# An encoder block with expert retrieval on one core: preparing the operands of the dense stage's products one tile earlier, with a third buffer for one pair of halves

## Chip, core and metric

One NeuronCore of a Trainium2 chip runs the whole program. The metric is the device time of one execution in microseconds. The profile is that of one further execution, taken by the hardware profiler; its times are counted from the first instruction of the span. Engines are called as in the profile: PE (TensorE matmul; PEld is its weight load), DVE (VectorE), ACT (ScalarE), POOL (GpSimd) and SP (SyncE, which here only issues transfers).

## The reference

One layer on 512 tokens of width 1024: modulation from `c`, an input projection, dilated and differential attention, gates, an output projection, and then PEER, a feed-forward part that picks 16 of 16384 single-neuron experts for each of 8 heads and each token. PEER is where the change lies:

```
q = (xc @ w_query).reshape(PEER_CHUNK, PEER_HEADS, 2, PEER_HALF)
... top 16 of the keys of either half, then of their 256 sums ...
eidx = e1 * PEER_N_KEYS + e2
gate = jax.nn.softmax(top, axis=-1)
u = expert_u[eidx]
vv = expert_v[eidx]
act = jax.nn.gelu(jnp.einsum('td,thkd->thk', xc, u).astype(jnp.float32), approximate=False)
wts = (gate * act).astype(xc.dtype)
return jnp.einsum('thk,thkd->td', wts, vv)
```

## The kernel before

The kernel computes PEER in two ways side by side. For 128 of the tokens it gathers the chosen rows of `expert_u` and `expert_v` from memory: 256 indirect transfers of 128 rows (512 KB each), issued by POOL into four buffers `gat`; DVE uses each once, as a dot product (`gscr`, L1065) or as a weighted sum (`acc`, L1077). For the other 384 tokens it works densely over all 16384 experts in 128 tiles of 128 experts: gelu(h2 u) for every expert, times the gate (zero for the experts that a token did not choose), times V. A matmul of two f32 operands is made of three: each operand is split into a high half, which ACT makes by a copy, and a low half, which DVE or POOL makes by subtracting (`split`, L91 and L92; `hi, lo` for weights, `ah, al` for activations), and PE multiplies high by high, high by low and low by high.

**The dense stage** is the loop at L1207, in the order of the list `order`: eight tiles whose activations are computed in the stage (e from 64 on: `stage_s` loads their `uT`, splits it, has PE do 24 products `pj`, and ACT apply gelu into `am`), then eight tiles whose activations were computed earlier in the program and stored (e below 64: `stage_s` loads `am` from `gls`), and so on, eight times. In this text tiles are numbered 0 to 127 in that order, and U is the `uT` of a tile and V its `expert_v`. `stage_s` runs LEAD = 4 tiles ahead, so that the 24 products of U for tile n+4 stand before the 18 products `y` of tile n. So the products of tiles 12 to 19, 28 to 35, 44 to 51 and so on come with a U each (here: a heavy stretch), and those of tiles 4 to 11, 20 to 27, 36 to 43 and so on without (a light stretch). The gathers and their uses are spread over the loop by `run_jobs(done)` at the end of each turn, twice as many for a tile with e from 64 on.

What a turn does for its own tile, before its products: multiply `am` by the gates `gch` (DVE, L1212), split the result into `ah` and `al` (two buffers each), load V (`w4`), and split it into `vh` and `vl`. V and U share the pool of `w4`: five buffers of either half, three of `raw`. `am` has four buffers. `gch` holds the gates of eight tiles (1.5 MB, two buffers) and is loaded by `stage_s` at the first tile of eight.

Five things set the order. PE, DVE, ACT and SP each take their instructions in the order that a scheduler of the language made of the source when the program was built, by the source's order and its own estimates; each engine then waits at an instruction until its operands and buffers are there. POOL is under `manual_schedule` in this loop and takes its instructions in the source's order. A load waits on SP for its buffer, and what is behind it on SP waits too.

Of the kernel before, what the change touches and what calls it, by code (L numbers as in the profile page):

```python
# [16 lines left out]
F32R = mybir.dt.float32r  # L17
# [5 lines left out]
OP = mybir.AluOpType  # L23
# [872 lines left out]
def peer(K, A, out):  # L896
    nc, cst, gen, Pool = K.nc, K.cst, K.gen, K.Pool
    small, f2, mm3, split, ident = K.small, K.f2, K.mm3, K.split, K.ident
    h2tok = K.h2tok
    gd, gls = A['gd'], A['gls']  # L900
    ND, NS = 384, 64
# [4 lines left out]
    pw, w4 = K.pw, K.w4  # L906
# [8 lines left out]
    def ptr():  # L915
        return pe_.tile([128, 512], F32, name="pt", bufs=2)

    def pg():
        return pe_.tile([128, 512], F32, name="pg", bufs=2)
# [49 lines left out]
    for c in range(4):  # L969
        pieces = []  # L970
        for k in range(0, 8, 2):
            raw, hi, lo = w4(wq[:, k:k + 2, 512 * c:512 * c + 512])
# [3 lines left out]
        for hc in range(2):  # L976
            h = 2 * c + hc
# [110 lines left out]
    def run_jobs(done):  # L1088
        while jobs and njobs - len(jobs) < done:
            jobs.pop(0)()  # L1090
# [14 lines left out]
    for b, a in enumerate(DT):  # L1105
# [3 lines left out]
        for n, t in enumerate(slots(gt, a)):  # L1109
            p = ptr()  # L1110
# [16 lines left out]
        for t0 in range(0, 128, T):  # L1127
# [15 lines left out]
            for q in range(0, T, 4):  # L1143
                p = pg()
# [21 lines left out]
    v = A['expert_v'].rearrange("(e p) d -> e p d", p=128)  # L1166
    py = Pool("py", space=PSUM)
    ys = [[py.tile([128, 512], F32, name=f"y{b}{n}") for n in range(2)] for b in range(3)]
    lp = Pool("main")
    gch, ams = {}, {}  # L1170

    def stage_s(e):
        if e % 8 == 0:
            gch[e // 8] = lp.tile([128, 12, 8, 32], F32, name="gch", bufs=2)
            nc.sync.dma_start(gch[e // 8].rearrange("p h e t -> p h (e t)"),
                              gd[e // 32][:, e // 8 % 4].rearrange("h p e t -> p h (e t)"))
        am = ams[e] = pa.tile([128, ND], F32, name="am", bufs=4)
        if e < NS:
            nc.sync.dma_start(am, gls[e])
        else:  # L1180
            gelu_s(e, pmat(), am, nc.gpsimd if e % 2 == 0 else nc.vector)


    order = []
# [3 lines left out]
    order = [8 * c + i for c in order for i in range(8)]  # L1188
# [3 lines left out]
    def residual(a):  # L1192
        for n in range(2):
            ns = slice(n * 512, n * 512 + 512)
            y = lp.tile([128, 512], F32, name="yo", bufs=6)
            nc.vector.tensor_tensor(y, acc[:, ns] if a == 0 else ys[a - 1][n], K.g2[:, ns], op=OP.mult)
            (nc.gpsimd if a in PR else nc.vector).tensor_tensor(y, y, xr[a][:, ns], op=OP.add)
            (nc.scalar if n else nc.sync).dma_start(ov[:, a, ns], y)
# [5 lines left out]
    pool_order = K.tc.manual_schedule(engines={mybir.EngineType.Pool})  # L1204
    pool_order.__enter__()
    done = float(J0)
    for n_, e in enumerate(order):  # L1207
        if n_ + LEAD < 128:
            stage_s(order[n_ + LEAD])
        am = ams.pop(e)  # L1210
        amv = am.rearrange("p (h t) -> p h t", t=32)
        nc.vector.tensor_tensor(amv, amv, gch[e // 8][:, :, e % 8, :], op=OP.mult)  # L1212
        ah = lp.tile([128, ND], F32R, name="ah", bufs=2)
        al = lp.tile([128, ND], F32R, name="al", bufs=2)
        split(ah, al, am)
        raw, vh, vl = w4(v[e])
        split(vh, vl, raw, nc.gpsimd if e % 4 == 1 else nc.vector)
        if n_ == 126:
            run_jobs(njobs)
            for a in range(4):  # L1220
                xr[a] = g0.tile([128, 1024], F32, name="gat", bufs=GB)
                nc.sync.dma_start(xr[a], A['x1d'][:, a, :])
            residual(0)
        for b in range(3):
            bs = slice(b * 128, b * 128 + 128)
            prods = [(i, n) for i in range(3) for n in range(2)]
            if n_ == 127:
                prods.sort(key=lambda t: t[1])
            for i, n in prods:
                l, r = ((ah, vh), (ah, vl), (al, vh))[i]  # L1230
                nc.tensor.matmul(ys[b][n], l[:, bs], r[:, n * 512:n * 512 + 512],  # L1231
                                 start=n_ == 0 and i == 0, stop=n_ == 127 and i == 2)
        done += (njobs - J0) * (1 if e < NS else 2) / (254.0 - NS)
        run_jobs(done)
# [14 lines left out]
def block(tc, A, out):  # L1249
    with ExitStack() as ctx:  # L1250
        dram = ctx.enter_context(tc.tile_pool(name="dram", bufs=1, space=bass.MemoryType.DRAM))
        A['x1d'] = dram.tile([128, 4, 1024], F32, name="x1d")
        A['gd'] = [dram.tile([12, 4, 128, 8, 32], F32, name=f"gd{c}") for c in range(4)]
        A['gls'] = dram.tile([128, 128, 384], F32, name="gls")
        A['sc0'] = dram.tile([128, 16, 128], F32, name="sc0d")
        K = Ctx()
        setup(tc, ctx, K)
        front(K, A)
        peer(K, A, out)
# [29 lines left out]
```

## Time and profile before

| | |
|---|---|
| median of three runs | 2042.31 us (2037.0 to 2042.57) |
| profiled execution | 2043.98 us, of which the span from first to last instruction is 2042.2 us |
| PE busy | 1918.3 us, 94% of the span |
| DVE, ACT, POOL busy | 78%, 41%, 40% |
| granted clock of PE, mean | 0.982 of full |
| moved by DMA | 436.80 MB, mean 214 GB/s |
| dense stage (first to last product `y`) | 1193.9 to 2034.9 us |

How to read it: a share of busy time is a mean over stages with different limits. A line of the timeline is start, duration, engine, source line, instruction, what it writes and reads, how many were merged, and in brackets the idle time of the engine before it with what ended that. The granted clock is a share of full speed: 1.00 is 2.4 GHz, 0.50 is 1.2 GHz. Successive products overlap in the listing (0.39 us each, one every 0.233 us).

### The profile page before, as it was taken

What the parts mean: (1) busy time and instruction counts of PE and PEld (TensorE: products, weight loads), DVE (VectorE), ACT (ScalarE), POOL (GpSimd) and SP (SyncE); (2) the same over time, 40 slices, a digit from 0 to 9 for tenths busy, and PEclk for the clock granted to TensorE, in tenths of its full rate; (3) what the DMA queues carried; (4) which work ended last, traced back from release to release, by engine and by line L of the source; (5) the groups of instructions that cost most, each with busy time, mean ns of one, the idle gap of its engine ahead of it and who ended that gap; (6) DMA issues with size and microseconds to landing.
All of it is one profiled execution on the core that took longest, in us unless ns stands there. A gap on an engine that the chain in (4) does not pass through costs nothing.

```text
span 2042.2 us, 28294 instructions
## 1 busy us (share of the span) xinstructions
PE 1918.3 (94%) x9858; PEld 1659.9 (81%) x9858; DVE 1585.0 (78%) x3212; ACT 844.9 (41%) x1330; POOL 821.9 (40%) x598
## 2 busy tenths in 40 slices
PE   6999999989899899999999998989898999999998
PEld 5987777777777788999999986968787878888886
DVE  8488585887766658998888778677877888878787
ACT  3444445646533333455666532333332333333232
POOL 2554332352244531000000545455555565746474
PEclk9999999999999899999999999999999999999999
DMA  7334142122246322646656998797979898989886
GB/s 261 90 115 123 52 145 57 37 84 87 63 150 213 140 88 88 190 151 214 225 194 209 336 340 310 272 338 257 357 280 323 288 331 299 338 291 327 320 318 256
DMA packets 199952, 436.80 MB, mean 214 GB/s; under 512 B 16465, under 2 KB 97666, under 8 KB 199682
## 3 DMA queue, kind: packets, MB, share of 16 engines
q1 hardware_dynamic: 162128, 298.65, 43.4%
q0 software_dynamic: 36864, 134.23, 18.0%
q10 hardware_dynamic: 818, 2.12, 0.3%
q8 instruction: 77, 1.26, 0.2%
q14 instruction: 65, 0.53, 0.1%
HBM read 391.95 MB, written 42.99 MB: 213 GB/s over the span
## 4 chain that ended last, share of the span: by engine, by line
PE 34%; DMA 19%; DVE 10%; issue 10%; POOL 5%; ACT 1%; SPq 0%; DVEq 0%; POOLq 0%; ACTq 0%
PE pj L86 6%; PE y L1231 6%; PE pj L87 6%; PE pj L88 6%; DMA gat<-expert_v,eidx 5%; PE pg L1147 5%; DMA raw<-uT 3%; DMA gat<-expert_u,eidx 3%; DMA am<-gls 3%; POOL gat L1059 3%; DVE wlo L92 2%; DMA raw<-expert_v 2%; POOL wlo L92 2%; PE pq L86 1%; PE pq L88 1%
## 5 line engine op out<-in xcount | busy, mean ns | idle before, releaser
L91 ACT ACTIVATE whi<-raw 128x1024 fp32r<-128x1024 f32 (+3 forms) x431 | 383.6, 894 | 610.4 <-DMA raw<-expert_v 242.6
L92 POOL TENSOR_TENSOR wlo<-raw,whi 128x1024 fp32r<-128x1024 f32 (+2 forms) x156 | 316.4, 2032 | 406.4 <-ACT whi L91 375.9
L92 DVE TENSOR_TENSOR wlo<-raw,whi 128x1024 fp32r<-128x1024 f32 (+3 forms) x275 | 333.7, 1217 | 136.5 <-ACT whi L91 136.1
L1059 POOL DMA_INDIRECT gat<-expert_u,eidx x128 | 162.6, 1270 | 464.6 <-DVE eidx L1125 343.5
L86 PE MATMUL pj<-h2h,whi 128*128 128x384 f32 x1008 | 344.4, 342 | 1.0 <-ACT am L879 1.0
L88 PE MATMUL pj<-h2h,wlo 128*128 128x384 f32 x1008 | 343.3, 341 | 0.0
L87 PE MATMUL pj<-h2l,whi 128*128 128x384 f32 x1008 | 343.3, 341 | 0.0
L1231 PE MATMUL y<-whi,al 128*128 128x512 f32 x768 | 239.3, 403 | 32.0 <-DVE al L92 32.0
L1231 PE MATMUL y<-wlo,ah 128*128 128x512 f32 x768 | 246.1, 401 | 9.2 <-POOL wlo L92 7.9
L1231 PE MATMUL y<-whi,ah 128*128 128x512 f32 x768 | 248.0, 400 | 5.5 <-ACT ah L91 5.4
L1059 POOL DMA_INDIRECT gat<-expert_v,eidx x128 | 172.8, 1350 | 132.8 <-DVE acc L1077 73.6
L1231 PEld LDWEIGHTS y<-whi,al 128*128 128x128 f32 x768 | 144.2, 190 | 76.7 <-DVE al L92 43.1
L1065 DVE SCALAR_TENSOR_TENSOR gscr<-gat,h2tok 128x1024 bf16<-128x1024 f32 x128 | 178.7, 1396 | 32.5 <-DMA gat<-expert_u,eidx 31.9
L86 PE MATMUL pj<-whi,hh 128*128 128x512 f32 (+2 forms) x512 | 193.0, 390 | 11.0 <-DVE gA L651 4.4
L1077 DVE SCALAR_TENSOR_TENSOR acc<-gat,wts,acc 128x1024 f32<-128x1024 f32 x127 | 173.9, 1369 | 31.6 <-DMA gat<-expert_v,eidx 31.1
L87 PE MATMUL pj<-wlo,hh 128*128 128x512 f32 (+2 forms) x512 | 196.0, 383 | 2.4 <-DVE wlo L92 2.3
L86 PEld LDWEIGHTS pj<-h2h,whi 128*128 128x128 f32 x1008 | 190.9, 189 | 4.2 <-ACT am L879 1.3
L87 PEld LDWEIGHTS pj<-h2l,whi 128*128 128x128 f32 x1008 | 190.7, 189 | 2.5
L88 PE MATMUL pj<-whi,hl 128*128 128x512 f32 (+2 forms) x512 | 192.0, 382 | 0.0
L88 PEld LDWEIGHTS pj<-h2h,wlo 128*128 128x128 f32 x1008 | 190.6, 189 | 0.4
L1231 PEld LDWEIGHTS y<-wlo,ah 128*128 128x128 f32 x768 | 146.6, 191 | 45.6 <-POOL wlo L92 8.3
L1231 PEld LDWEIGHTS y<-whi,ah 128*128 128x128 f32 x768 | 145.2, 191 | 36.8 <-ACT ah L91 7.3
(313 smaller groups left out, 3207.8 us busy)
## 6 DMA issues: line engine op xcount, KB each, us to landing
raw<-uT SPq DMA_DIRECT2D x128, 512.0 KB, 4.4
raw<-expert_v SPq DMA_DIRECT2D x128, 512.0 KB, 6.2
gd<-stage SPq DMA_DIRECT2D x48, 512.0 KB, 4.4
gch<-gd SPq DMA_DIRECT2D x16, 1536.0 KB, 11.2
raw<-w_in SPq DMA_DIRECT2D x88, 256.0 KB, 2.8
raw<-w_ada SPq DMA_DIRECT2D x64, 256.0 KB, 2.8
am<-gls SPq DMA_DIRECT2D x64, 192.0 KB, 6.2
gls<-am SPq DMA_DIRECT2D x62, 192.0 KB, 2.0
```

What stands on the lines that cost most here:

```text
L86: nc.tensor.matmul(ps, lh, rh, start=start, stop=False)
L87: nc.tensor.matmul(ps, lh, rl, start=False, stop=False)
L88: nc.tensor.matmul(ps, ll, rh, start=False, stop=stop)
L91: nc.scalar.activation(hi, raw, AF.Copy)
L92: (eng or nc.vector).tensor_tensor(lo, raw, hi.bitcast(F32), op=OP.subtract)
L1059: nc.gpsimd.indirect_dma_start(out=t, out_offset=None, in_=src, in_offset=bass.IndirectOffsetOnAxis(ap=eidx[:, s:s + 1], axis=0))
L1065: nc.vector.scalar_tensor_tensor(scr, t, 1.0, h2tok, op0=OP.mult, op1=OP.mult, accum_out=act[:, s:s + 1])
L1077: nc.vector.scalar_tensor_tensor(acc, t, wts[:, s:s + 1], acc, op0=OP.mult, op1=OP.add)
L1147: nc.tensor.matmul(p[:, j * 128:j * 128 + 128], oh[1][:, :, q + j], pcs[i][:, :, q + j], start=i == 0, stop=i == 1)
L1231: nc.tensor.matmul(ys[b][n], l[:, bs], r[:, n * 512:n * 512 + 512], start=n_ == 0 and i == 0, stop=n_ == 127 and i == 2)
```

## The change

What a turn did for its own tile it now does for the next one: the gating of `am`, the split into `ah` and `al`, the load of V and its split stand in a function `prepare`, called once for tile 0 ahead of the loop and then in turn n for tile n+1, between `stage_s` of tile n+4 and the products of tile n. `ah` and `al` have three buffers each. The counts and shapes of all instructions and transfers are the same.

```diff
@@ -1204,17 +1204,27 @@
     pool_order = K.tc.manual_schedule(engines={mybir.EngineType.Pool})
     pool_order.__enter__()
     done = float(J0)
+    ready = {}
+
+    def prepare(n):
+        e = order[n]
+        am = ams.pop(e)
+        amv = am.rearrange("p (h t) -> p h t", t=32)
+        nc.vector.tensor_tensor(amv, amv, gch[e // 8][:, :, e % 8, :], op=OP.mult)
+        ah = lp.tile([128, ND], F32R, name="ah", bufs=3)
+        al = lp.tile([128, ND], F32R, name="al", bufs=3)
+        split(ah, al, am)
+        raw, vh, vl = w4(v[e])
+        split(vh, vl, raw, nc.gpsimd if e % 4 == 1 else nc.vector)
+        ready[n] = ah, al, vh, vl
+
+    prepare(0)
     for n_, e in enumerate(order):
         if n_ + LEAD < 128:
             stage_s(order[n_ + LEAD])
-        am = ams.pop(e)
-        amv = am.rearrange("p (h t) -> p h t", t=32)
-        nc.vector.tensor_tensor(amv, amv, gch[e // 8][:, :, e % 8, :], op=OP.mult)
-        ah = lp.tile([128, ND], F32R, name="ah", bufs=2)
-        al = lp.tile([128, ND], F32R, name="al", bufs=2)
-        split(ah, al, am)
-        raw, vh, vl = w4(v[e])
-        split(vh, vl, raw, nc.gpsimd if e % 4 == 1 else nc.vector)
+        if n_ + 1 < 128:
+            prepare(n_ + 1)
+        ah, al, vh, vl = ready.pop(n_)
         if n_ == 126:
             run_jobs(njobs)
             for a in range(4):
```

DVE's queue at the start of a light stretch, before: from the gating of tile 37 (`am_14193`) to `al` of tile 36 (`al_14408`). `al_14366` is that of tile 35; each row L1077 is the use of one gathered buffer.

```order
L1212 TENSOR_TENSOR am_14193<-am_14193,gch_13857 128x384
L1077 SCALAR_TENSOR_TENSOR acc_7898<-gat_14393,wts_7900,acc_7898 128x1024
L92 TENSOR_TENSOR al_14366<-am_14057,ah_14365 128x384
L1077 SCALAR_TENSOR_TENSOR acc_7898<-gat_14396,wts_7900,acc_7898 128x1024
L92 TENSOR_TENSOR wlo_14411<-raw_14413,whi_14412 128x1024
L1077 SCALAR_TENSOR_TENSOR acc_7898<-gat_14399,wts_7900,acc_7898 128x1024
L1077 SCALAR_TENSOR_TENSOR acc_7898<-gat_14435,wts_7900,acc_7898 128x1024
L1212 TENSOR_TENSOR am_14260<-am_14260,gch_13857 128x384
L1077 SCALAR_TENSOR_TENSOR acc_7898<-gat_14438,wts_7900,acc_7898 128x1024
L92 TENSOR_TENSOR al_14408<-am_14122,ah_14407 128x384
```

The same queue and place in the changed program: from the gating of tile 37 (`am_14204`) over `al` of tile 36 (`al_14377`) to `al` of tile 37 (`al_14419`).

```order
L1213 TENSOR_TENSOR am_14204<-am_14204,gch_13868 128x384
L1077 SCALAR_TENSOR_TENSOR acc_7898<-gat_14333,wts_7900,acc_7898 128x1024
L92 TENSOR_TENSOR al_14377<-am_14133,ah_14376 128x384
L1077 SCALAR_TENSOR_TENSOR acc_7898<-gat_14336,wts_7900,acc_7898 128x1024
L92 TENSOR_TENSOR wlo_14380<-raw_14382,whi_14381 128x1024
L1077 SCALAR_TENSOR_TENSOR acc_7898<-gat_14339,wts_7900,acc_7898 128x1024
L1077 SCALAR_TENSOR_TENSOR acc_7898<-gat_14404,wts_7900,acc_7898 128x1024
L1213 TENSOR_TENSOR am_14271<-am_14271,gch_13868 128x384
L1077 SCALAR_TENSOR_TENSOR acc_7898<-gat_14407,wts_7900,acc_7898 128x1024
L92 TENSOR_TENSOR al_14419<-am_14204,ah_14418 128x384
```

Where `al` of tile 35 stood there now stands that of tile 36, and where that of tile 36 stood, that of tile 37. Counted from the first gather of the program, `al` of tile 36 stood behind 89 uses and now stands behind 82.

SP's queue in the same light stretch, before: the loads of stored activations of tiles 40 and 41 (`am_14404`, `am_14441`) and the gates `gch` of the eight tiles from 48 on.

```order
L799 DMA raw_14601<-expert_v 128x1024
L1179 DMA am_14404<-gls_62 128x384
L799 DMA raw_14638<-expert_v 128x1024
L1175 DMA gch_14697<-gd2_60 128x12x256
L1179 DMA am_14441<-gls_62 128x384
L799 DMA raw_14672<-expert_v 128x1024
L1179 DMA am_14481<-gls_62 128x384
```

The same in the changed program (`am_14415` and `am_14452` are tiles 40 and 41, `am_14492` is tile 42):

```order
L799 DMA raw_14578<-expert_v 128x1024
L1179 DMA am_14415<-gls_62 128x384
L1179 DMA am_14452<-gls_62 128x384
L799 DMA raw_14612<-expert_v 128x1024
L1175 DMA gch_14708<-gd2_60 128x12x256
L1179 DMA am_14492<-gls_62 128x384
L799 DMA raw_14649<-expert_v 128x1024
```

The activations of tile 41 stood behind the gates and now stand ahead of them; the first load behind the gates is now that of tile 42.

## Rows read from the trace of the kernel before

**Rows 1.** The page: busy time, share of the span and instructions of each engine, and the busy share of the DMA engines, in tenths, in 40 equal slices of the span.

```profile
PE 1918.3 (94%) x9858; PEld 1659.9 (81%) x9858; DVE 1585.0 (78%) x3212; ACT 844.9 (41%) x1330; POOL 821.9 (40%) x598
DMA  7334142122246322646656998797979898989886
```

**Rows 2.** Busy time by stretch of the dense stage, light and heavy in turn: stretch and its length, busy time and instructions of PE, PEld, DVE, ACT and POOL, granted clock, busy share of the DMA engines, GB/s.

```profile
1447.00:1488.00 41.00, 34.62 (x146) 26.75 (x145) 35.22 (x40) 12.54 (x18) 22.17 (x16) 1.00 0.97 354
1488.00:1559.00 71.00, 71.00 (x353) 63.64 (x352) 57.34 (x64) 25.95 (x37) 42.00 (x27) 1.00 0.84 291
1559.00:1596.00 37.00, 31.57 (x128) 24.57 (x127) 27.12 (x32) 9.11 (x13) 16.61 (x12) 0.95 0.96 348
1596.00:1663.00 67.00, 67.00 (x336) 60.41 (x336) 51.09 (x60) 23.38 (x32) 41.51 (x24) 1.00 0.81 284
```

**Rows 3.** Who waited for whom from 1190 us on: total us, times, longest.

```profile
PE y L1231 <- DVE al L92: 32.0, 22, 3.8
PE y L1231 <- POOL wlo L92: 7.9, 1, 7.9
PE y L1231 <- ACT ah L91: 5.4, 2, 4.2
PE y L1231 <- DVE wlo L92: 1.3, 1, 1.3
DVE am L1212 <- DMA am<-gls: 32.2, 8, 8.6
ACT ah L91 <- PE y L1231: 104.0, 50, 4.1
```

**Rows 4.** PE in the light stretch of tiles 36 to 43 (products with `al` of tiles 36 and 37, the first with the low half of V of tile 38, those with `al` of tiles 38, 40 and 42).

```profile
1449.57 0.73 PE L1231 MATMUL y<-whi,al 128*128 128x512 f32 x2 [1.92 <-DVE al L92]
...
1457.51 1.20 PE L1231 MATMUL y<-whi,al 128*128 128x512 f32 x4 [2.31 <-DVE al L92]
...
1460.17 0.63 PE L1231 MATMUL y<-wlo,ah 128*128 128x512 f32 x2
...
1463.47 1.68 PE L1231 MATMUL y<-whi,al 128*128 128x512 f32 x6 [0.80 <-DVE al L92]
...
1472.56 1.21 PE L1231 MATMUL y<-whi,al 128*128 128x512 f32 x4 [1.35 <-DVE al L92]
...
1481.07 1.09 PE L1231 MATMUL y<-whi,al 128*128 128x512 f32 x4
```

**Rows 5.** DVE in the same stretch (from the use that is number 86 of the program to `al` of tile 36, the low half of V of tiles 38 and 39, `al` of tile 37, the gating of tile 41).

```profile
1440.30 1.28 DVE L1077 SCALAR_TENSOR_TENSOR acc<-gat,wts,acc 128x1024 f32<-128x1024 f32 x1
...
1442.63 4.75 DVE L1077 SCALAR_TENSOR_TENSOR acc<-gat,wts,acc 128x1024 f32<-128x1024 f32 x2
...
1447.76 1.28 DVE L1077 SCALAR_TENSOR_TENSOR acc<-gat,wts,acc 128x1024 f32<-128x1024 f32 x1
1448.96 0.56 DVE L92 TENSOR_TENSOR al<-am,ah 128x384 fp32r<-128x384 f32 x1
1449.43 1.22 DVE L92 TENSOR_TENSOR wlo<-raw,whi 128x1024 fp32r<-128x1024 f32 x1
...
1452.90 1.22 DVE L92 TENSOR_TENSOR wlo<-raw,whi 128x1024 fp32r<-128x1024 f32 x1
...
1456.90 0.55 DVE L92 TENSOR_TENSOR al<-am,ah 128x384 fp32r<-128x384 f32 x1
...
1471.48 0.56 DVE L1212 TENSOR_TENSOR am<-am,gch 128x384 f32<-128x384 f32 x1 [2.54 <-DMA am<-gls]
```

**Rows 6.** SP in the same stretch, and the gating of tile 57 in the light stretch after the next (its gates `gch` were issued at 1560.69, third row).

```profile
1455.81 0.38 SPq L1175 DMA_DIRECT2D gch<-gd  x1
1457.48 0.33 SPq L1179 DMA_DIRECT2D am<-gls  x1
1560.69 0.38 SPq L1175 DMA_DIRECT2D gch<-gd  x1
1578.52 0.56 DVE L1212 TENSOR_TENSOR am<-am,gch 128x384 f32<-128x384 f32 x1 [8.59 <-DMA am<-gls]
```

**Rows 7.** Stretches behind waits of PE at a lower clock: one after the wait for the low half of V of tile 9, one after a wait for `al`, and the sum of four of 3.4 us each after waits for `al` (from 1353.8, 1579.1, 1674.7 and 1889.7 us; each with a granted clock of 0.50); columns as in rows 2.

```profile
1248.00:1254.80 6.80, 3.82 (x9) 3.05 (x10) 6.77 (x6) 0.00 (x0) 2.90 (x2) 0.50 0.65 226
1579.10:1582.50 3.40, 2.90 (x7) 2.33 (x8) 3.40 (x4) 1.47 (x2) 0.36 (x1) 0.50 0.47 114
...
sum 13.60, PE 13.10 PEld 10.25 DVE 6.51 ACT 3.05 POOL 5.40; mean PE 3.28 PEld 2.56 DVE 1.63 ACT 0.76 POOL 1.35
```

**Rows 8.** Durations and transfers in the dense stage: the chain's piece of 18 products of one tile; low halves on DVE and on POOL and high halves on ACT (min/median/max ns); loads of U with the median us from issue to landing; the last two gathers on POOL ahead of the low half of V of tile 9.

```profile
1483.92 4.20 PE y L1231 x18
L92 DVE TENSOR_TENSOR wlo<-raw,whi x124: 1208/1217/3955, 1200.3 to 2019.2; 128x1024 fp32r<-128x1024 f32 x124
L92 POOL TENSOR_TENSOR wlo<-raw,whi x60: 2345/2422/3763, 1201.2 to 2010.3; 128x1024 fp32r<-128x1024 f32 x60
L91 ACT ACTIVATE whi<-raw x182: 1041/1061/1066, 1199.5 to 2013.8; 128x1024 fp32r<-128x1024 f32 x182
raw<-uT SPq DMA_DIRECT2D x56, 512.0 KB, 5.2
1246.01 1.01 POOL L1059 DMA_INDIRECT gat<-expert_u,eidx  x1 [0.60 <-DVE gscr L1065]
1247.62 0.94 POOL L1059 DMA_INDIRECT gat<-expert_u,eidx  x1 [0.60 <-DVE gscr L1065]
```

## The prediction

> **What bounds the kernel now.** I read the page first: PE is busy for 94% of the span [rows 1], so only its idle time and its slow time can be won. By the diff this is about the dense stage, 1194 to 2035 us. The table by stretch splits that in two kinds. In a heavy stretch, where each tile's 18 products come with 24 of a U, PE has no idle time (71.00 of 71.00, 67.00 of 67.00) and the DMA engines are 81 to 84% busy. In a light stretch, products alone, PE is idle for 6.4 of 41 and 5.4 of 37 us, and DMA is at 96 to 97% [rows 2]. A light tile costs PE 4.2 us [rows 8]; 336 products in 67.0 us [rows 2] make 8.4 us for a heavy one.
>
> The waits say for what PE is idle: 32.0 us in 22 waits for `al`, 7.9 in one for a low half of V made by POOL, 5.4 for `ah` (4.2 of them the first product of the stage) and 1.3 for one more low half of V; 46.6 us together [rows 3].
>
> The timelines say why `al` is late. In the light stretch of tiles 36 to 43 PE waits 1.92, 2.31, 0.80 and 1.35 us for it, 6.38 in all [rows 4]. DVE is not idle meanwhile: `al` of tile 36, made at 1448.96, has three uses of gathered buffers right ahead of it, the pair from 1442.63 taking 4.75 us [rows 5]. V is not late: the low half of tile 38 is done at 1449.43 + 1.22 = 1450.65 [rows 5] and first used at 1460.17 [rows 4], 9.5 us spare. So what PE lacks is a 0.55 us instruction that stands in DVE's queue behind uses whose gathers come over a full DMA. A second cause feeds it: DVE waits 32.2 us in 8 waits for stored activations [rows 3]. Those of tile 41 were issued 1.7 us after the 1.5 MB of gates `gch`, and the gating of tile 41 could start 1471.48 - 1455.81 = 15.7 us after the gates' issue; for tile 57 it was 17.8 us [rows 6]. In DVE's queue that gating stands ahead of `al` of tile 40, for which PE then waits.
>
> The waits also cost clock. Behind four of these stretches the granted clock is 0.50 for 3.4 us each, with 13.1 us of PE work in it, and behind the 7.9 us wait for 6.8 us, with 3.8 us of work [rows 7].
>
> **The change part by part.** It removes no instruction and no byte, and the engines' shares stay. What it can change is order and buffers.
>
> *`al` in DVE's queue.* Counted in the two orders, `al` of tile 36 moves from behind 89 uses to behind 82, tile 37 from 92 to 86, 38 from 94 to 89, 40 from 95 to 91; in the other light stretches it is 3 to 9 uses. The 86th use ended at 1440.30 + 1.28 = 1441.6 [rows 5]. PE wants `al` of tile 37 at 1457.51 [rows 4], and 4.23 us earlier, at 1453.3, without the first two waits: 11.7 us spare if the gathers come no faster than now. So this bound removes all the 32.0 us; the other bound is that something else comes just as late (rivals), and removes nothing. I take 30 of 32.0, since the first bound is met with room.
>
> *Third buffer of `ah` and `al`.* The split of tile n+2 waited for the products of tile n, 104.0 us of waits [rows 3]; it now waits for those of tile n-1. This lets the line above happen. Queued behind a split that waits are gather uses, which have the spare time just named.
>
> *Stored activations.* The load of tile 41 now stands ahead of the gates, and the first behind them is tile 42's. The V load ahead of the gates reuses the `raw` of tile 39, whose low half on DVE (1452.90 [rows 5]) moves from behind 89 uses to behind 86, so the gates can go some us earlier than 1455.81. Even at 1455.81 + 17.8 = 1473.6 the load of tile 42 meets a need of 1481.07 - 6.38 = 1474.7 [rows 4], less 1.6 us for gating and two splits (0.56 and 0.55 [rows 5], and a copy on ACT that I estimate at half of V's 1.06 [rows 8]): 0.5 us late if the gates do not move, 7 or more us in time if they move by 8. I price it at zero beyond the 2 us kept above.
>
> *Clock.* 13.1 us of work at half speed [rows 7] is 6.5 us lost; with the waits gone I take back 5.5.
>
> *V of tile 9.* Its low half is made by POOL, in the source's order, and stood behind the 38th gather; now behind the 36th. The last two were issued 1247.62 - 1246.01 = 1.6 us apart [rows 8], so 3.2 us of the 7.9 go at most; I take 3. The other 31 splits of V on POOL also move ahead of one to three gathers. Behind a split that waits stand the gathers, whose uses have room; zero.
>
> *U against V in the pool of halves.* This is the cost. Source order takes the five buffers as U(n+4), V(n+1) where it was U(n+4), V(n), while PE's order stays U(n+4), then tile n. A U took over the buffer of an item with four items of PE work still ahead of it, 16.8 us; now with two, 8.4 us, at the tightest. After the buffer is free it needs the high half (1.06 us) and the low half (1.22 on DVE, 2.42 on POOL) [rows 8]: 2.3 to 3.5 us, hidden. That cover is gone if the load itself comes late: 5.2 us to landing [rows 8] make it 7.5 to 8.7 us, and one use ahead of it on DVE (1.28 [rows 5]) 8.8 to 10.0, that is up to 1.6 us late. Ends: 0, and 56 U [rows 8] x 1.6 = 90 us. The load writes `raw`, which has three buffers of its own and frees earlier, so I take 2 us.
>
> **Sum.** -30 - 5.5 - 3 + 2 = -36.5 us. The profiled execution took 2043.98 us, 1.7 more than the median of the runs: 2043.98 - 36.5 = 2007.5, say 2008, which leaves the difference to the median in hand.
>
> **Rivals.** *The stored activations are late next.* If the gates go out no earlier while PE runs ahead, tile 42 and its likes wait 2 to 3 us in each of six stretches (0.5 by the count above, and as much more as PE has gained before it) and the clock keeps falling: 6 x 2.3 + 5.5 = 19 us of the gain are lost, 2027. For it: 32.2 us of waits for these loads now [rows 3]. Against: one load fewer is behind the gates.
>
> *No change, DMA is the bound.* A light stretch moves 41 us x 354 GB/s = 14.5 MB [rows 2]. At that rate 34.6 us (without the waits) carry 12.2 MB, so 2.3 MB must leave the stretch or the waits only get another name: 2042. Against: 4 to 7 uses of 0.5 MB now stand behind the `al` that they preceded, 2.1 to 3.7 MB, and a heavy stretch has 71 x (354 - 291) = 4.5 MB of room [rows 2]. The Trainium skill speaks for this rival (Trainium Kernel Development and Optimization, Key Constraints): transfers issued from SP, ACT and POOL run on the same 16 DMA engines and interleave, so a new order within SP's queue takes no share from POOL's gathers. The 96 to 97% agree with it [rows 2]; by that rule alone the sum would be near zero, by the rows with their room it is the -36.5 above.
>
> *Slower, U late.* In heavy stretches, where PE has no idle time [rows 2], U's halves come up to 1.6 us late: +90 - 38.5 = +51, 2095. It decides from 38.5 / 56 = 0.7 us per U on; at half its price the time is 2050. For it: U's lead is halved. Against: `raw` frees earlier than the halves, and loads of U land in 5.2 us at the median.
>
> **How the numbers follow.** Chances: the forecast 0.56 (1997 to 2018: all of the 46.6 us but the first 4.2, or 10 us less than the sum), stored activations late 0.22 (2018 to 2034), no change 0.09, U late 0.10 (2049 up), better than the forecast's range 0.03. Leaving out no more than 0.2: 1997 to 2036. A measurement of this kernel can tell about 0.3%, 6 us, from no change: faster 0.81, the same 0.09, slower 0.10.
>
> **What would show it.** Right: PE's wait for `al` falls from 32.0 to a few us; `al` stands ahead of its product by 5 us or more in light stretches; ACT's wait of `ah` for products falls from 104.0; light stretches go at 4.2 us a tile, with DMA still near 96%, and heavy ones get a higher DMA share; the granted clock stays at 1.00 behind tiles 24, 56, 72 and 104. Wrong: waits of PE for halves of U in heavy stretches (`pj` behind `whi` or `wlo`), which the trace before does not have at all; or the same idle time of PE in light stretches under `am<-gls` or the halves of V.

## The result and the profile after

The changed kernel takes 2055.37 us (median of 6 runs, 2049.67 to 2060.24), the kernel before 2040.78 us (6 runs, 2036.62 to 2042.57): a ratio of 1.007 with a 95% interval of 1.0055 to 1.0086. It is slower by 0.7%, where 1.6% faster was forecast. The profiled execution of the changed kernel took 2052.16 us, its span 2050.3 us.

The page of the changed kernel, its first part and the busy share of the DMA engines in 40 slices:

```profile
PE 1911.6 (93%) x9858; PEld 1656.7 (81%) x9858; DVE 1573.3 (77%) x3212; ACT 848.1 (41%) x1330; POOL 829.1 (40%) x598
DMA  7344141132255333646565998898888797979887
```

The shares are those of [rows 1]. What changed is who waits for whom (changed kernel, from 1190 us on):

```profile
PE y L1241 <- POOL wlo L92: 45.9, 7, 13.1
DVE am L1213 <- DMA am<-gls: 42.0, 7, 8.3
PE y L1241 <- ACT whi L91: 6.8, 2, 3.5
PE pj L88 <- POOL wlo L92: 1.6, 2, 0.9
PE pj L88 <- DVE wlo L92: 0.9, 2, 0.5
ACT ah L91 <- PE y L1241: 158.3, 66, 11.6
```

Against [rows 3]: the 32.0 us for `al` are gone, there is no such row any more. In their place the wait for a low half of V made by POOL grew from 7.9 us in one to 45.9 us in seven. The dense stage, from the first product `y` to the last, in the kernel before and in the changed one (columns as in rows 2):

```profile
1193.80:2035.00 841.20, 798.62 (x3696) 680.57 (x3696) 674.67 (x747) 273.10 (x378) 477.45 (x301) 0.99 0.86 307
```

```profile
1185.50:2039.00 853.50, 798.13 (x3696) 684.54 (x3696) 659.71 (x742) 275.92 (x378) 478.84 (x299) 0.97 0.85 304
```

The stage is 12.3 us longer with the same PE time (798.6 and 798.1), so it is all idle time. It starts 8.3 us earlier, of which 6.2 us are PE being busy for less time ahead of the stage with the same instructions (1918.3 - 798.6 against 1911.6 - 798.1). The start of the stage lies anywhere from 1189 to 1196 us in the profiles of the eleven other kernels below, so its share is not put down to the change. From the last product to the end it is 11.4 us where it was 7.3. -8.3 + 12.3 + 4.1 = +8.1 us is the difference of the two profiled spans; the medians are 14.6 us apart, and of what is beyond the 8.1 no profile tells.

All seven waits are in light stretches, one in each but the last, at the tile that is the sixth of its stretch: 9, 25, 41, 57, 73, 89 and 105. The light stretch of tiles 20 to 27 in the changed kernel: first SP (the gates; the load of tile 26's activations), then DVE, POOL and PE:

```profile
1333.67 0.37 SPq L1175 DMA_DIRECT2D gch<-gd  x1
1335.52 0.32 SPq L1179 DMA_DIRECT2D am<-gls  x1
...
1343.27 0.55 DVE L92 TENSOR_TENSOR al<-am,ah 128x384 fp32r<-128x384 f32 x1
1350.63 0.56 DVE L1213 TENSOR_TENSOR am<-am,gch 128x384 f32<-128x384 f32 x1 [6.81 <-DMA am<-gls]
1351.11 1.28 DVE L1077 SCALAR_TENSOR_TENSOR acc<-gat,wts,acc 128x1024 f32<-128x1024 f32 x1
...
1343.62 1.01 POOL L1059 DMA_INDIRECT gat<-expert_u,eidx  x1 [1.92 <-DVE acc L1077]
1352.65 1.68 POOL L1059 DMA_INDIRECT gat<-expert_u,eidx  x1 [8.02 <-DVE acc L1077]
1354.35 2.61 POOL L92 TENSOR_TENSOR wlo<-raw,whi 128x1024 fp32r<-128x1024 f32 x1
...
1349.98 1.56 PE L1241 MATMUL y<-whi,ah 128*128 128x512 f32 x6
1357.01 1.22 PE L1241 MATMUL y<-wlo,ah 128*128 128x512 f32 x2 [5.48 <-POOL wlo L92]
```

Read from the bottom: PE waits for the low half of V of tile 25. V was there; its high half was done at 1335.2. But POOL takes its instructions in order, and ahead of the subtraction stands a gather that waits 8.02 us for a buffer, that is for the use at 1351.11 on DVE. DVE takes its instructions in order too, and ahead of that use stands the gating of tile 26, which waits 6.81 us for a load issued 1.9 us behind the 1.5 MB of gates. So a load of 192 KB for tile 26 holds the product of tile 25, by way of DVE, a gather's buffer and POOL. (Trainium skill, Perfetto Trace Analysis, Sequencer Loop: a sequencer takes the next instruction, and that one waits for its semaphores. The rows agree: DVE does nothing from 1343.8 to 1350.6, though the gather of the use behind had landed at 1343.77.)

Light and heavy stretches of the changed kernel, and the first 3.4 us behind that wait:

```profile
1333.00:1370.00 37.00, 31.52 (x128) 25.00 (x127) 28.36 (x38) 9.45 (x14) 16.22 (x12) 0.91 0.86 309
1370.00:1437.00 67.00, 67.00 (x337) 60.49 (x336) 52.11 (x59) 24.90 (x34) 43.83 (x27) 1.00 0.86 304
...
1357.00:1360.40 3.40, 3.39 (x8) 2.74 (x9) 3.40 (x6) 0.52 (x1) 1.03 (x1) 0.50 0.98 299
```

The light stretch has lost its idle time for `al` and has one wait instead, and the granted clock falls to 0.50 (1.2 GHz) behind it, as it did behind the waits of [rows 7]. The heavy stretch is at full rate, as before [rows 2].

The tail is new too. Pieces of the chain that ended last in the changed kernel:

```profile
2022.55 1.61 POOL wlo L92
2025.80 1.76 POOL gat L1059
2027.86 8.09 DMA gat<-expert_v,eidx
2036.04 1.30 DVE acc L1077
```

The last use of a gathered buffer ends at 2037.3; before it ended at 2022.5, 12.4 us ahead of the last product. The result of the gathered tokens is now what the end waits for: the 4.1 us.

### The profile page after: what moved, and what is told of

Read it like the earlier page. It is cut to its first block, busy times and chain, and to the rows that moved or that the text cites. A ratio compares the mean times of both kernels' runs of the same rounds, so it can differ in the third digit from the quotient of the medians.

```text
span 2050.3 us, 28275 instructions
## 1 busy us (share of the span) xinstructions
PE 1911.6 (93%) x9858; PEld 1656.7 (81%) x9858; DVE 1573.3 (77%) x3212; ACT 848.1 (41%) x1330; POOL 829.1 (40%) x598
## 4 chain that ended last, share of the span: by engine, by line
PE 38%; DMA 13%; issue 10%; DVE 10%; POOL 6%; ACT 2%; SPq 0%; DVEq 0%; POOLq 0%; ACTq 0%
PE pj L86 7%; PE pj L87 7%; PE pj L88 7%; PE y L1241 7%; DMA gat<-expert_v,eidx 5%; PE pg L1147 4%; POOL gat L1059 3%; DMA raw<-expert_v 3%; DMA gat<-expert_u,eidx 3%; POOL wlo L92 2%; DVE wlo L92 2%; DVE acc L1077 2%; PE pq L86 1%; PE pq L88 1%; PE pq L87 1%
## 5 line engine op out<-in xcount | busy, mean ns | idle before, releaser
L92 DVE TENSOR_TENSOR wlo<-raw,whi 128x1024 fp32r<-128x1024 f32 (+3 forms) x275 | 315.3, 1154 | 115.1 <-ACT whi L91 114.9
L1059 POOL DMA_INDIRECT gat<-expert_u,eidx x128 | 167.9, 1312 | 469.8 <-DVE eidx L1125 343.7
L1241 PE MATMUL y<-wlo,ah 128*128 128x512 f32 x768 | 251.9, 407 | 45.9 <-POOL wlo L92 45.9
L1241 PE MATMUL y<-whi,al 128*128 128x512 f32 x768 | 248.3, 404 | 0.0
L1241 PE MATMUL y<-whi,ah 128*128 128x512 f32 x768 | 234.1, 396 | 8.4 <-ACT whi L91 6.8
L1077 DVE SCALAR_TENSOR_TENSOR acc<-gat,wts,acc 128x1024 f32<-128x1024 f32 x127 | 183.2, 1442 | 27.7 <-DMA gat<-expert_v,eidx 26.9
L1065 DVE SCALAR_TENSOR_TENSOR gscr<-gat,h2tok 128x1024 bf16<-128x1024 f32 x128 | 173.6, 1357 | 25.1 <-DMA gat<-expert_u,eidx 24.1
L91 ACT ACTIVATE ah<-am 128x384 fp32r<-128x384 f32 x128 | 66.7, 523 | 286.7 <-PE y L1241 158.3
L1241 PEld LDWEIGHTS y<-whi,al 128*128 128x128 f32 x768 | 148.5, 194 | 35.3
```

The lines of the kernel that those rows point to most:

```text
L91: nc.scalar.activation(hi, raw, AF.Copy)
L92: (eng or nc.vector).tensor_tensor(lo, raw, hi.bitcast(F32), op=OP.subtract)
L1059: nc.gpsimd.indirect_dma_start(out=t, out_offset=None, in_=src, in_offset=bass.IndirectOffsetOnAxis(ap=eidx[:, s:s + 1], axis=0))
L1065: nc.vector.scalar_tensor_tensor(scr, t, 1.0, h2tok, op0=OP.mult, op1=OP.mult, accum_out=act[:, s:s + 1])
L1077: nc.vector.scalar_tensor_tensor(acc, t, wts[:, s:s + 1], acc, op0=OP.mult, op1=OP.add)
```

## Experiments

Each is an edit of the changed kernel but `b_v9_dve`. Ratios are against the kernel before on the same chip.

**V of tile 9, 25, ... on DVE.**

```diff
-        split(vh, vl, raw, nc.gpsimd if e % 4 == 1 else nc.vector)
+        split(vh, vl, raw, nc.gpsimd if e % 4 == 1 and n % 16 != 9 else nc.vector)
```

> The changed kernel, with the low half of V of tiles 9, 25, 41 and so on (n % 16 == 9; 8 of the 128 tiles) made by DVE instead of POOL. Theory A (PE's 45.9 us of waits for a low half on POOL come from POOL's queue: that subtraction stands behind gathers, which wait for uses that DVE holds back): the 45.9 us in 7 waits fall to under 10, what takes their place on DVE is at most 1 to 2 us per light stretch, and the time is 2055 - 36 - 5 of clock = about 2014, at least below 2030. Rival B (the gathers and loads over the full DMA set the pace of a light stretch, and the wait only gets another name): PE's idle time in the dense stage stays within 10 us of 57, under another releaser, and the time is 2045 to 2060.

2004.4 us, ratio 0.9827 (0.9808 to 0.9847). Eight of 60 subtractions moved, and by the ratios the kernel is 2.4% faster than the changed one. Waits, and two light stretches:

```profile
DVE am L1213 <- DMA am<-gls: 33.6, 8, 7.2
PE pj L88 <- DVE wlo L92: 18.9, 2, 9.8
```

```profile
1332.00:1366.00 34.00, 34.00 (x148) 27.41 (x147) 27.17 (x39) 11.43 (x17) 17.01 (x12) 1.00 1.01 377
1635.00:1669.00 34.00, 34.00 (x148) 27.43 (x147) 26.12 (x33) 11.40 (x16) 16.83 (x11) 1.00 0.98 354
```

Theory A holds: no wait for POOL is left, though DVE still waits for the loads, and the time is some 10 us better than it said. Rival B falls: these stretches run with no idle time of PE at all. The DMA engines are hardly faster for it. In the six light stretches of tiles 20 to 107, each taken from its first product `y` to the first `pj` behind it, they move 73.1 MB at 363 GB/s, where the kernel before moved 78.0 MB at 354 GB/s. These stretches are 18.5 us shorter in sum, and at 354 GB/s the 4.9 MB less make 13.8 us of that; the heavy ones behind them run at 292 to 325 GB/s where they had 276 to 299.

**The gates in halves.**

```diff
-        if e % 8 == 0:
-            gch[e // 8] = lp.tile([128, 12, 8, 32], F32, name="gch", bufs=2)
+        if e % 4 == 0:
+            gch[e // 4] = lp.tile([128, 12, 4, 32], F32, name="gch", bufs=4)
...
```

The lines cut are the load and the gating, which take their four tiles accordingly.

> The changed kernel, with the gates loaded for four tiles at a time (0.75 MB, four buffers, the same memory) instead of eight (1.5 MB, two buffers): of the 1.5 MB that went out in a light stretch ahead of the stored activations, half moves into the heavy stretch before. Theory A2 (the head of the chain is DVE waiting for stored activations that lie behind the gates on the way): DVE's wait for them, 42.0 us in 7, falls to under 20, PE's wait for low halves on POOL from 45.9 to under 25, and the time to 2025 to 2040. Rival (POOL's gathers are late for the DMA's own pace, whatever DVE waits for): DVE's wait falls but PE's 45.9 stays above 35, and the time stays at 2050 to 2060.

2037.5 us (10 runs, 2029.89 to 2047.61), ratio 0.9988 (0.9963 to 1.0013).

```profile
DVE am L1213 <- DMA am<-gls: 38.7, 14, 6.0
PE y L1241 <- POOL wlo L92: 33.5, 5, 12.5
```

In between. The time is in the range of A2, but not for its reason: DVE's wait in sum hardly fell (38.7, under 20 expected), it was cut into 14 shorter ones, PE's wait stayed above the 25 expected, and three of the seven stretches came free (tiles 25, 41 and 89). The size of the lump matters, but it does not say which stretch is held.

**Each half of the change alone.** In `act_alone` the load and split of V stand in the tile's own turn again, after `ready.pop`:

```diff
-        raw, vh, vl = w4(v[e])
-        split(vh, vl, raw, nc.gpsimd if e % 4 == 1 else nc.vector)
-        ready[n] = ah, al, vh, vl
+        ready[n] = ah, al
...
-        ah, al, vh, vl = ready.pop(n_)
+        ah, al = ready.pop(n_)
+        raw, vh, vl = w4(v[e])
+        split(vh, vl, raw, nc.gpsimd if e % 4 == 1 else nc.vector)
```

In `v_alone`, in the same way, gating and split of the activations do, with `bufs=2`; V stays ahead.

> One half of the change alone: gating and split of the activations one tile ahead with three buffers, V loaded and split in its own tile's turn as before (so U and V take the buffers of the halves in the old order). Theory A: the waits for al are gone (32.0 to under 3) and PE waits for the low half of tiles 9, 25 and so on made by POOL as in the whole change or worse, since that subtraction stands one tile's gathers later: 45 to 65 us, time 2050 to 2065. Rival C (what costs is V ahead: the order of U and V in the buffers): PE's idle time falls by 25 us or more against the kernel before, time 2010 to 2030.

2010.1 us, ratio 0.9859 (0.9841 to 0.9878).

```profile
DVE am L1213 <- DMA am<-gls: 30.3, 11, 7.8
PE y L1241 <- POOL wlo L92: 8.1, 1, 8.1
PE y L1241 <- ACT ah L91: 8.0, 3, 4.4
PE y L1241 <- DVE al L92: 1.5, 2, 1.2
```

> The other half alone: load and split of V one tile ahead, gating and split of the activations in their own turn with two buffers. Theory A: the waits for al stay (25 to 35 us), the one for V of tile 9 on POOL (7.9 us) shrinks or stays, the gathers are ordered as in the whole change; time 2035 to 2048. Rival C (V ahead costs by itself, through U's lead in the buffers and the splits on POOL that hold the gathers): waits of PE for halves of U or V in heavy stretches, 10 us or more, and the last use of a gathered buffer 10 us or more later than before (2022.5): time above 2050.

2068.3 us, ratio 1.0147 (1.0122 to 1.0173).

```profile
DVE am L1223 <- DMA am<-gls: 50.0, 7, 8.4
PE y L1241 <- POOL wlo L92: 31.0, 7, 11.2
PE y L1241 <- DVE al L92: 12.4, 5, 3.3
PE y L1241 <- ACT whi L91: 6.0, 2, 3.2
PE pj L86 <- ACT whi L91: 5.9, 3, 2.4
PE pj L88 <- POOL wlo L92: 2.7, 2, 1.8
PE pj L88 <- DVE wlo L92: 1.5, 1, 1.5
```

Theory A missed both. Activations alone gain nearly all that was forecast, and POOL's subtraction, one tile's gathers later in its queue, holds PE in the first stretch only. V alone loses. Rival C's numbers came true in both: in `act_alone` PE is idle for 27.7 us less in the stage than in the kernel before and the time is at the lower edge of the range; `v_alone` is above 2050, with the last use at 2053.6. So moving V ahead is what costs. But most of the cost does not come by rival C's way: waits for high halves of V and for halves of U, in heavy stretches, make some 16 us in `v_alone`, those for POOL in light ones 31.0. So a subtraction that stands earlier in POOL's queue is ready later, which neither theory had. What tells the kernels apart is a count (theory D). There are four gather buffers, so what stands behind G gathers on POOL needs G - 4 uses on DVE. If the gating that waits for the late load stands behind fewer uses than that, the load holds POOL. Counted in the two orders, with PE's wait for POOL from the traces, for the six stretches from the second on:

| kernel | V made by POOL, uses needed | tile of the late gating, uses ahead of it | PE's wait, us |
|---|---|---|---|
| before | 25, ...: 64 94 125 155 185 216 | 25, ...: 64 95 125 156 186 216 | none |
| changed | 25, ...: 63 93 123 154 184 214 | 26, ...: 62 92 121 152 182 212 | 5.5 1.6 6.2 8.7 3.1 7.8 |
| `act_alone` | 25, ...: 64 94 125 155 185 216 | 26, ...: 64 95 126 156 186 217 | none |
| `v_alone` | 25, ...: 63 93 123 154 184 214 | 25, ...: 62 92 121 152 182 212 | 1.7 1.7 0.3 8.3 2.8 4.9 |

The change moved the subtraction forward by one or two gathers, but the gating of tiles 26, 42, 58 and so on by four to six uses (from 66, 97, 127, 158, 188, 218). Done alone, activations ahead leave the two where they do not cross. In `v_alone` the source has the gatings where they were, and the scheduler still put that of tile 25 behind 62 uses instead of 64; why was not followed. The count was read off after the fact, so the next three kernels were made to test it.

**V of tile 8, 24, ... on POOL in place of 9, 25.** The test that keeps POOL's work as it is.

```diff
-        split(vh, vl, raw, nc.gpsimd if e % 4 == 1 else nc.vector)
+        split(vh, vl, raw, nc.gpsimd if e % 4 == 1 and n % 16 != 9 or n % 16 == 8 else nc.vector)
```

> The changed kernel, with POOL making the low half of V of tiles 8, 24, 40 and so on in place of 9, 25, 41: POOL and DVE have as much work as in the changed kernel. Theory D (a count in two queues): POOL's subtraction behind G gathers needs G - 4 uses on DVE, since there are four buffers; if fewer uses than that stand ahead of the gating of tile 10, 26 and so on, which waits for its late load, the load holds POOL and PE. In the changed kernel G - 4 is 63, 93, 123, 154 for tiles 25, 41, 57, 73, and the gating of the next tile stands behind 62, 92, 121, 152 uses: held in all. Here it is 60, 90, 121, 151 for tiles 24, 40, 56, 72, and the gating of 26, 42, 58, 74 stands behind 61, 92, 122, 152: held nowhere but in the first stretch (30 against 27). So PE's wait for low halves on POOL falls from 45.9 to under 12, and the time to 2000 to 2018, as with the subtraction on DVE. Rival E (POOL's subtraction is too slow for a light stretch, 2.4 to 4.4 us instead of 1.2, or POOL has too much work): the waits stay, for tile 8 now and larger, since PE wants it 4.2 us earlier: 50 us or more, time 2050 or above.

2013.5 us (2007.43 to 2024.01), ratio 0.9856 (0.9813 to 0.9899).

```profile
PE y L1241 <- POOL wlo L92: 14.0, 2, 13.8
PE pj L88 <- POOL wlo L92: 8.5, 5, 2.8
```

As the count says: 13.8 of the 14.0 us are in the first stretch, the one that was named, though PE wants this tile 4.2 us sooner; the sum is above the 12 that was set. Rival E falls: in the other stretches the same subtraction on POOL costs next to nothing. New are 8.5 us for halves of U made by POOL.

**The count at its edge.** `act_alone` with POOL on tile 10, 26, ... in place of 9, 25:

```diff
-        split(vh, vl, raw, nc.gpsimd if e % 4 == 1 else nc.vector)
+        split(vh, vl, raw, nc.gpsimd if e % 4 == 1 and n_ % 16 != 9 or n_ % 16 == 10 else nc.vector)
```

> Activations alone ahead, as in act_alone, with POOL making the low half of V of tile 10, 26 and so on in place of 9, 25: the count of theory D at its edge. Uses needed against uses ahead of the gating of the same tile: tile 10 35 against 29, tile 26 65 against 64, tile 42 96 against 95, tile 90 187 against 186: held until after that gating. Tile 58 126 against 126, 74 156 against 156, 106 217 against 217, 122 247 against 247: not held. Theory D: where DVE waits 2 us or more for the load, POOL's subtraction starts 2 us or more after the gating's start in tiles 10, 26, 42 and 90, and no more than one use and one gather after it, or before it, in 58, 74 and 106. Rival E: no such difference between the two groups. Time 2005 to 2025.

2016.6 us in one run. DVE's gating and POOL's subtraction for tile 26, one use short, and for tile 58, with none short:

```profile
1353.40 0.56 DVE L1213 TENSOR_TENSOR am<-am,gch 128x384 f32<-128x384 f32 x1 [8.74 <-DMA am<-gls]
1357.82 2.38 POOL L92 TENSOR_TENSOR wlo<-raw,whi 128x1024 fp32r<-128x1024 f32 x1
...
1562.88 0.56 DVE L1213 TENSOR_TENSOR am<-am,gch 128x384 f32<-128x384 f32 x1 [6.59 <-DMA am<-gls]
1557.13 2.41 POOL L92 TENSOR_TENSOR wlo<-raw,whi 128x1024 fp32r<-128x1024 f32 x1
```

In tile 26 POOL starts 4.4 us after the gating, in 42 and 90 3.0 us after it; in 58, 74 and 106 it starts 5.8, 6.1 and 2.5 us before it. In these six, DVE waited 4.1 to 8.7 us. Theory D has all six right, and one use decides; in tiles 10 and 122 DVE did not wait, so they tell nothing. Over the six stretches from the second on in the kernel before, the changed one, `act_alone`, `v_alone`, `v8_pool`, this one and the next, POOL's subtraction starts after the late gating where the count is short and before it where it is not, in 42 of 42 stretches. Where the count is short, that follows from the order of the two queues alone; what the traces add is that it starts before where the count is not short.

The count does not say what a held subtraction costs. `gates_half`, which is not among the 42, shows that: the count is short in all six of its stretches, and POOL starts 3.0 to 7.5 us after the late gating, but PE waits only in the three where DVE waited 5.2 to 6.0 us for the load (7.8, 9.95 and 2.96 us). Where DVE waited 2.6 to 3.5 us, the subtraction still came in time.

**More lead for the loads.**

```diff
-        am = ams[e] = pa.tile([128, ND], F32, name="am", bufs=4)
+        am = ams[e] = lp.tile([128, ND], F32, name="am", bufs=8)
```

> The changed kernel, with eight buffers instead of four for the activations in the dense stage, so that the loads of the stored ones go out up to four tiles earlier: the loads of tiles 24 to 29 now stand ahead of the gates on SP, and the first one behind them is that of tile 30. Rival G (the cause is simply a load that is issued too late for its tile: give it more lead and the wait is gone): DVE's wait for stored activations falls from 42 us to under 10, PE's wait for low halves on POOL from 45.9 to under 10, time 2005 to 2020. Theory D (the count): the scheduler moves the gatings up as far as the loads, so the gating of tile 30 stands behind 62 uses, 46 behind 92, 62 behind 122, 78 behind 152, 110 behind 213, and V of tiles 25, 41, 57, 73, 105 still needs 63, 93, 123, 154, 214: held as before, now by a tile that PE wants much later; only tile 89 (184 needed, 184 ahead) goes free. PE's wait for low halves on POOL stays at 30 to 50 us, time 2035 to 2060.

2048.6 us (10 runs, 2043.89 to 2057.33), ratio 1.003 (1.0006 to 1.0054). PE's wait in the six stretches is 3.3, 4.3, 6.3, 7.4, 0.7 and 6.5 us, 39.7 in all with 10.7 in the first and 0.4 in the last. Tiles 25 (held by the gating of tile 30) and 89 (free by the count):

```profile
1352.41 0.56 DVE L1213 TENSOR_TENSOR am<-am,gch 128x384 f32<-128x384 f32 x1 [3.86 <-DMA am<-gls]
1355.47 2.51 POOL L92 TENSOR_TENSOR wlo<-raw,whi 128x1024 fp32r<-128x1024 f32 x1
...
1791.17 0.56 DVE L1213 TENSOR_TENSOR am<-am,gch 128x384 f32<-128x384 f32 x1 [5.27 <-DMA am<-gls]
1787.13 2.39 POOL L92 TENSOR_TENSOR wlo<-raw,whi 128x1024 fp32r<-128x1024 f32 x1
```

Rival G falls: with four tiles more lead a later gating stands at the same place and waits, and DVE's wait for stored activations is 41.6 us, where rival G had under 10. In the one stretch that was to go free POOL starts 4.0 us ahead of the gating, and PE waits 0.7 us.

**Control: the kernel before with V of tile 9, 25, ... on DVE,** by the edit of `v9_dve`, with `n_` for `n`.

> The kernel before, with only the low half of V of tile 9, 25, 41 and so on made by DVE instead of POOL: the control for the changed kernel with the same edit. By the count, POOL holds PE in the kernel before at tile 9 alone (7.9 us and the half clock behind it), so theory D gives 2041 - 8 - 2 = 2031, 2025 to 2038, with the waits for al still near 32 us. Rival F (the edit helps in itself, for POOL's gathers go faster without those eight subtractions, whatever the change does): 2015 or below, and waits for al under 20 us.

2029.8 us, ratio 0.9946 (0.9927 to 0.9965), the time that theory D gave.

```profile
PE y L1231 <- DVE al L92: 20.5, 15, 3.7
PE y L1231 <- POOL wlo L92: 0.5, 1, 0.5
```

On top of that edit the change is worth 0.9827 / 0.9946 = 0.988, some 24 us. The waits for `al` are not near the 32 expected but close to the 20 that rival F named, though its time of 2015 is far off. Why was not followed further.

**Towards a better kernel.** Three more. `act_v9_dve` is `act_alone` with the edit of `v9_dve`; the other two are `v9_dve` with another share of gathers per turn:

```diff
-        done += (njobs - J0) * (1 if e < NS else 2) / (254.0 - NS)
+        done += (njobs - J0) * (2 if order[min(n_ + LEAD, 127)] >= NS else 1) / (254.0 - NS)
```

```diff
-        done += (njobs - J0) * (1 if e < NS else 2) / (254.0 - NS)
+        done += (njobs - J0) * (1 if e < NS else 2) / (248.0 - NS)
```

> Activations alone ahead, and the low half of V of tiles 9, 25 and so on made by DVE: of the 8.1 us that PE still waits for POOL there (tile 9 alone) and of the 6 us after it at half clock nothing is left. Theory A and D: 2010 - 8 - 2 = 2000, 1994 to 2006. Rival (DVE gets 8 times 1.2 us in light stretches and becomes late itself): 2008 or above, with new waits of PE for low halves made by DVE.

2012.0 us (2000.04 to 2016.7), ratio 0.9867 (0.9825 to 0.9909), above the range and where the rival had it. The profile is that of the fastest of five runs, 2000.04 us; PE waits 6.4 us in it for `ah`, 5.5 for low halves of V made by DVE, the rival's sign, 4.5 for `al` and 1.2 for U. Where the other runs lose their 12 us, it doesn't show.

> The changed kernel with V of tile 9, 25 and so on split by DVE, and the double share of gathers given to the turns whose U is computed (tile n + 4 with e from 64 on) instead of the turns with e from 64 on: the same 256 gathers, eight to twelve of them per period moved from light stretches into heavy ones, where PE has no idle time and the DMA engines 16 to 19% of room. If light stretches are still paced by the DMA (rival B): DMA share in light stretches falls below 0.90 and the 20 us of idle time that PE has left in the dense stage fall below 8, time 1988 to 1998. If not: 2000 to 2010, or above where the heavy stretches then run late with halves of U.

2016.4 us, ratio 0.987 (0.9825 to 0.9915). The three light stretches looked at have DMA shares of 0.95 to 0.99, and the heavy ones 21.6 us of waits for halves of U (11.3 for high halves, 10.3 for low halves made by POOL), the last of the outcomes named. It gained nothing: the light stretches of `v9_dve` had no idle time left to give.

> The changed kernel with V of tile 9, 25 and so on split by DVE, and all gathers spread over the first 97% of the stage (the divisor of the share per tile 248 - 64 instead of 254 - 64), meant to take the end of the gathers off the chain that ended last: in that kernel the last use of a gathered buffer ended at 1994.0, 3.7 us before the last product, and 12.5 us before the end. Expected: last use 5 us or more further ahead of the last product, the end 7 to 8 us after the last product instead of 8.7 or more, 1 to 4 us gained: about 2002, 1994 to 2008. If 3% more gathers in each stretch bring back waits of PE: 2010 or above.

2021.7 us, ratio 0.9895 (0.9864 to 0.9927), the outcome named for waits that come back. In the profiled execution, the slowest of six (2032.88 us), the last use did come earlier, 18 us ahead of the last product, but a wait that `v9_dve` has in two heavy stretches grew:

```profile
PE pj L88 <- DVE wlo L92: 33.8, 6, 11.3
```

The low half of the second U of a heavy stretch stands on DVE behind uses, as `al` did; this is also the 18.9 us left in `v9_dve`. Of all kernels `v9_dve` has the lowest ratio; `act_alone`, without a third change, is 0.3% behind it with intervals that overlap. Both beat the kernel before and the changed one.

## Why the prediction was wrong

*`al` in DVE's queue: right.* 32.0 us to none, by the count of uses that was given, and 30 were taken. *Third buffer: not tested by itself, and its sign failed.* ACT's wait of `ah` for products rose from 104.0 to 158.3 us where it was to fall. With activations alone ahead it did fall, to 60.8; `v9_dve`, the fastest, has 150.5, so this wait does not tell what PE loses.

*V of tile 9: this is the step that failed.* -3 us was taken, by counting that the split moves ahead of two gathers, and zero for the other splits on POOL, since gathers behind them have room. Measured: from 7.9 to 45.9 us, +38.0, of which +5.2 are at tile 9 and +32.8 at the six other tiles. The step counted what stands ahead of the split and what stands behind it, not what the gathers ahead wait for. Each needs a use, and in the new order the gating of the next tile, which waits for a load, had come ahead of those uses as well as `al`. The prediction counted `al` against uses in DVE's order, and never the gating, nor the uses against POOL's order. [Rows 6] had shown that such a gating starts 15.7 and 17.8 us after the gates go out. That the queues cross is what costs is shown by `v9_dve`, `v8_pool` and `act_v10_pool`; the 5.2 us more at tile 9 are in part open, since the wait there was not understood before either.

*Stored activations: the load was right, its victim wrong.* The first load behind the gates is now that of tile 42, as said, and DVE's wait rose from 32.2 to 42.0 us. It was priced by when tile 42's own product is due. The tile hurt is 41, whose operands were all loaded. The rival of late stored activations, which made tile 42 wait, gave 2027.

*Clock: nothing came back.* 5.5 us were taken, and PE's time in the stage is the same within 0.5 us: seven waits, most of them long, cost the clock as much as 22 short ones. Without them it is 786.9 us in `v9_dve`, 11.7 less, and 790.7 in `act_alone`, 7.9 less: the term was sound, and if anything too small.

*U against V in the halves: right in size for the changed kernel.* 2 us were taken, 2.5 measured for halves of U. Another 6.8 us are for a high half of V, at the third tile of two heavy stretches. ACT waits 9.0 and 6.0 us there for a load of V issued 0.5 us behind the gates, so these are not the pool's. The rival of late U with 2095 is not what happened. But with POOL's waits gone, U is what is left to wait for: 18.9 us in `v9_dve`, while `act_alone`, with U and V in the old order, has 1.1.

*DMA as the bound: this rival fell, by `v9_dve`,* and for the reason set against it: 4.9 MB of six light stretches went elsewhere, at nearly the same rate. The Trainium skill's rule (Trainium Kernel Development and Optimization, Key Constraints) that transfers of all queues interleave on the same engines is not touched by that; what did not follow from it is a sum near zero.

*Not thought of:* the end of the gathers, 15 us later than before, and with it the last 4.1 us. The held subtractions are not all of it: in `v9_dve` the last use ends only 3.7 us ahead of the last product, where it was 12.4 before.

*Added up,* PE's idle time in the stage: -32.0 for `al`, +38.0 for POOL, +2.5 for U, +6.8 for high halves of V and -2.5 for `ah` and other low halves, together +12.8; less 0.5 of work, that is the +12.3 us by which the stage is longer.

## What to carry to other kernels

When work moves forward in an in-order queue, list everything that moves with it, and for each what it waits for; then ask which instructions on other engines now stand, through a buffer's release, behind that wait. With rotating buffers it is a count: an instruction behind G transfers into B buffers needs G - B releases, and a late load that stands ahead of one of them holds it. Whether that costs time depends on how late the load is and when the product is due. A split given to an engine that also issues such transfers inherits all their waits, so what is due soon does not belong there.

## What the runs showed of the hardware

The DMA engines' busy share did not tell whether PE would wait. In `v9_dve` PE has no idle time in the light stretches from the second on, at shares from 0.95 to 1.01 and 340 to 377 GB/s; in the two of the kernel before in [rows 2] it has some 15% at 0.96 to 0.97 and 348 to 354 GB/s. POOL's subtraction, 2.4 us at the median [rows 8], took 4.4 us for tile 73, in the changed kernel and in `v_alone`; PE's waits of 8.7 and 8.3 us contain it.

Left open: why POOL is late in the first stretch (8.1 us in `act_alone`, where DVE did not wait for a load ahead of it), and why `al` waits less in the control. For the first, `act_alone` gives a hint that no run tested: DVE is busy for 53.0 of the 60 us from 1195 on, and POOL's gathers there wait mostly for its uses.
